# Layer 0's output projection by the seven-product scheme, and layer 1 begun with the second token half

## The chip, the cores and the metric

The program runs on one core of one Trainium2 chip. The metric is the device time of one execution in microseconds; the time of a kernel is the median of its runs. TensorE (PE) does the matmuls, VectorE (DVE), ScalarE (ACT) and GpSimd (POOL) everything between them, and SyncE (SP) issues most of the DMAs.

## What is computed

A decoder trunk of two layers over 1024 tokens of width 1024, all in float32. Each layer normalises, projects to eleven groups of columns, runs four mLSTM heads and four retention heads of width 256 in chunks, gates and normalises their outputs, and projects 2048 columns back to 1024:

```python
for l in range(DEPTH):                                   # DEPTH = 2
    ada = c_act @ w_ada[l] + b_ada[l]
    shift, scale, gate = jnp.split(ada, 3, axis=-1)
    h = rmsnorm(x, norm_g[l]) * (1.0 + scale[:, None, :]) + shift[:, None, :]
    p = h @ w_in[l]
    mq, mk, mv, mo, mz, mi, mf, rq, rk, rv, rz = split_cols(p)
    ...                                                  # conv, rotary, mLSTM and retention by chunks
    y_m = jax.nn.sigmoid(mo) * head_layernorm(cell, gn_m[l], N_HEADS_MLSTM) * jax.nn.silu(mz)
    y_r = head_layernorm(ret, gn_r[l], N_HEADS_RET) * jax.nn.silu(rz)
    y = jnp.concatenate([y_m, y_r], axis=-1) @ w_out[l]  # (1024, 2048) @ (2048, 1024)
    x = x + gate[:, None, :] * y
return rmsnorm(x, final_g)
```

The change is about the product with `w_out[0]`, the residual and the norm behind it, and the first projections of layer 1.

## The kernel before

**Numbers in two parts.** A float32 operand is split into a high part (rounded to the PE's format by ACT, a `CAST`) and the rest (a subtraction on DVE or POOL). One product of a 128x128 block with a 128x512 block is then three matmuls, `mm3`: high by high (L177), high by rest (L178), rest by high (L179). The buffers are pools: `b` has 59 tiles of 128x512, `acc` 12, `wH` 5 (high parts of weights), `R` 12 (raw weights and their rests). PSUM has eight banks of 128x512: four by `ps_p()` (named px and pz in the profile) and four by `ps_a()` (pa).

**Order.** PE's instructions stand in the order in which the program is written. The other engines are ordered by a scheduler at build time, except what goes through `late`, which keeps its place. Work beside the main stream is written as generators: `launch(gen, delay)` starts one, `tick()` is called after each unit of matmuls, and `yield n` waits for n ticks. So `yield` numbers and the table of steps `TABLE` decide where in PE's stream such work stands.

**The input projections** are done in pairs by a scheme of seven products instead of eight half-sized ones (`pair_product`, `vpair_product`): sums and differences of weight blocks and of blocks of the input (`build_forms`, by DVE at the start of a layer), seven products, and sums of their results. A `Feeder` loads, adds and splits weights some slots before each product.

**Attention.** `attention` runs the steps of `TABLE` for a head, one entry per tick: q, k, d, t, v are loads, Q, K, s splits, S scores, V values, U state updates. `gate_chain` makes the mLSTM gates at the start of each layer: cumulative sums on DVE, four transposes by PE (L562) of a tile T4, and a transfer through DRAM (`mdr`). `gate_rows` (layer 1 only) makes the gate row of the last residual; its matmul is L345.

**Layer 0's output projection.** `out_units(0, half, cc, ...)` makes, for one token half (512 tokens) and one half `cc` of the output columns, four banks of 128 columns x 512 tokens, in 16 units over k (128 input columns each) of four `mm3`: 4 x 16 x 4 x 3 = 768 matmuls. The order of the four quarters is (half 0, cc 0), (half 0, cc 1), (half 1, cc 0), (half 1, cc 1). `OutLoads` loads a weight block per unit, and for cc 0 also the normalised output and the gate of that k; DVE multiplies them (L1258), ACT scales and splits (L1261), DVE makes the rest (L1262), and the split tiles are kept for cc 1. The rest of a weight block (L408) goes to DVE for cc 0 and to POOL for cc 1. When a bank is done, `column_evac` adds it, times the gate, to the residual (L1309, DVE), squares it on ACT and adds up the squares (L1315, POOL, in the last quarter DVE).

**Into layer 1.** `norm_later` sums the squares over partitions by PE (L1372), makes the root on POOL, spreads it by PE (L1384) and scales the eight tiles of the half (DVE L144 for half 0, L1391 for half 1; ACT L1392, L1393; POOL L1394). Half 0's runs under the projection of half 1. Layer 1 begins with `first`: three column blocks of the input projection, 72 matmuls for half 0 (L1484, L1485, L1488) and then 72 for half 1, whose norm runs under those of half 0.

Of the kernel before, what the change touches and what calls it, by code (L numbers as in the profile page):

```python
# [12 lines left out]
F32R = mybir.dt.float32r  # L13
# [74 lines left out]
def tile_hybrid_trunk(ctx, tc, x, xt, c, positions, w_ada, b_ada, norm_g, w_in, w_blk, w_val, conv_w, conv_b,  # L88
# [20 lines left out]
    def bt(dt=F32, n=512):  # L109
        return big.tile([P, n], dt, tag="b", name=nm("b"))  # L110
# [219 lines left out]
    def gate_rows(l):  # L330
        for half in range(2):
            accs = []
            yield from ada_rows(l, 2 * D + half * 512, accs)
            brow = wt("acc", 512, NACC)
            Q.dma_start(brow[0:1, :], b_ada[l, 2 * D + half * 512:2 * D + (half + 1) * 512].unsqueeze(0))
            yield 1
            acc = accs[0]
            V.tensor_tensor(acc[0:1, :], acc[0:1, :], brow[0:1, :], ALU.add)
            yield 1
            a2 = (wt("wH", 512, NW, F32R), wt("R", 512, NR, F32R))  # L340
            split_to(a2, acc)
            yield 2
            pt = ps_a()
            for i in range(2):
                PE.matmul(pt, ones_r, a2[i], start=i == 0, stop=i == 1)  # L345
# [13 lines left out]
    def gate_cols(l, gcol):  # L359
        for half in range(2):  # L360
            accs = []
            yield from ada_rows(l, 2 * D + half * 512, accs)
            yield 2
            pt = ps_a()
            for i in range(4):
                PE.matmul(pt[:, i:i + 1], accs[0][:, i * P:(i + 1) * P], ones, start=True, stop=True)
            V.tensor_tensor(gcol[:, 4 * half:4 * half + 4], pt[:, 0:4],
                            cols[l][0][:, 120 + 4 * half:124 + 4 * half], ALU.add)
            yield 1
# [133 lines left out]
    def gate_chain(l, pgs, gt):  # L503
# [459 lines left out]
    def load_rotary(rot):  # L963
        for which in range(2):
            for i in range(2):
# [5 lines left out]
    busy = [False]  # L971
    TABLE = ("q0 k0 d0 t0", "", "v0", "Q0 K0 m0 d1", "s0 k1", "S0", "m1 q1 K1", "v1", "Q1", "V001 t1", "S1 k2 q2", "U01",
             "s1 d2 K2", "v2 Q2", "V10 U2 m2", "S2", "t2 d3", "V11 U3 k3", "s2 q3", "v3 K3", "Q3 m3", "V20 U4",
             "S3", "", "V21 U5", "", "", "", "V30", "V31", "")
# [328 lines left out]

    def column_evac(gcol, xn, sq, keep):
        def evac(half, cc, i, bank):
            ct = cc * 4 + i
            xr = bt()
            Q.dma_start(xr, xt[ct * P:(ct + 1) * P, half * HALF:(half + 1) * HALF])
            V.scalar_tensor_tensor(xr, bank, gcol[:, ct:ct + 1], xr, ALU.mult, ALU.add)  # L1309
            if ct == 0:  # L1310
                A.activation(sq, xr, AF.Square)
            else:
                o = wt("acc", 512, NACC)
                A.activation(o, xr, AF.Square)
                (V if half and cc else G).tensor_tensor(sq, sq, o, ALU.add)  # L1315
            xn[ct] = xr
            if cc == 0:
                keep(ct)
        return evac

# [38 lines left out]
    def row_rstd(ss, tag, rows=(0, 1, 2, 3)):  # L1359
# [6 lines left out]
        return [rs[:, tt:tt + 1] for tt in range(n)]  # L1366

    def norm_later(l, xn, sq, hT, half, keep, gaps):
        yield gaps[0]
        pt = ps_a()  # L1370
        for i in range(4):
# [4 lines left out]
        G.tensor_tensor(rs, s, mhalf, ALU.pow)  # L1376
        dg = bt()
        V.tensor_tensor(dg.rearrange("p (a b) -> p a b", a=4), ident.unsqueeze(1).to_broadcast([P, 4, P]),
                        rs.unsqueeze(2).to_broadcast([P, 4, P]), ALU.mult)
        for ct in range(4, KT):  # L1380
            keep(ct)
        yield gaps[1]
        pr = ps_a()
        PE.matmul(pr, f(ones_r), dg, start=True, stop=True)  # L1384
        R = bt()
        A.copy(R, pr)
        yield gaps[2]
        for k in range(KT):
            gain, shift = gsh[l][:, 0, k:k + 1], gsh[l][:, 1, k:k + 1]
# [76 lines left out]
    for l in range(DEPTH):  # L1466
# [10 lines left out]

        def first(half, k, parts=(0, 1)):
            hH, hL = hT[k][half]
            for i, w in enumerate(wf):  # L1480
                if 0 in parts:
                    if k == 0:
                        pf[i][half] = ps_p() if i < 2 else ps_a()
                    PE.matmul(pf[i][half], w[k][0], hH, start=k == 0, stop=False)  # L1484
                    PE.matmul(pf[i][half], w[k][1], hH, start=False, stop=False)  # L1485
            for i, w in enumerate(wf):
                if 1 in parts:
                    PE.matmul(pf[i][half], w[k][0], hL, start=False, stop=k == KT - 1)  # L1488

# [76 lines left out]
        else:  # L1566
            gr = gate_raw(l)
            for half in range(2):
                for k in range(KT):
                    first(half, k)  # L1570
                    tick()
                if half == 0:
                    drain()
                    wg = gate_weights(gr)
        for half in range(2):
# [55 lines left out]
        going, forms, left = {}, {}, {}  # L1631
        loads = OutLoads(l)
        for j, n, part in slots:
            left[j] = left.get(j, 0) + 1
        for j, n, part in slots:
# [6 lines left out]
            tick()  # L1642
            if sum(left.values()) == 5:
                loads.fetch(2)
            elif sum(left.values()) == 3:
                loads.make()
            left[j] -= 1
            if left[j] == 0 and jobs[j][0] == "k":
                launch(attention(l, jobs[j][1][0], gt), 4, 1)
        nhT = [[None, None] for _ in range(KT)]  # L1650
        if l == DEPTH - 1:
# [4 lines left out]
            for cc in range(2):  # L1656
                t = bt()
                Q.dma_start(t, final_g[cc * 512:(cc + 1) * 512].unsqueeze(0).to_broadcast([P, 512]))
                V.tensor_scalar(t, t, math.sqrt(D), None, ALU.mult)
                fg.append(t)  # L1660
        for half in range(2):
            if l < DEPTH - 1:
                xn, sq = [None] * KT, bt()
                keep = keep_rows(half, xn)
                evac = column_evac(gcol, xn, sq, keep)
                run_units(out_units(l, half, 0, loads, evac))
                run_units(out_units(l, half, 1, loads, evac, 2 if half else 0))
                launch(norm_later(l + 1, xn, sq, nhT, half, keep, (1, 2, 0) if half else (3, 3, 11)))
                continue
            xn = [[None, None] for _ in range(4)]  # L1670
# [46 lines left out]
```

## Time and profile before

| | us |
|---|---|
| median of three runs | 2266.18 (2264.73 to 2269.15) |
| the profiled execution | 2268.18 |
| its span in the profile | 2266.5 |
| PE, DVE, ACT, POOL busy | 2151.5, 1817.5, 1159.4, 964.3 |
| layer 0's output projection in the profile | 970 to 1161 |
| layer 1's `first` | 1161 to 1195 |
| mean granted PE clock | 0.979 |

A row of a view names line, engine, operation and tiles without their numbers; `b<-acc,cols,b` is a tile of the pool b made from three operands. A PE row's duration is from issue to the modelled end and overlaps its neighbours, so the pace of PE is read from the starts of rows that follow each other.

### The profile page before, as it was taken

The page shows a single profiled execution, that of the slowest core. Times are in us where ns is not written, and L with a number is a line of the kernel's source. Part 1 is how long each engine was busy: PE and PEld are TensorE (multiplying, and loading weights), DVE is VectorE, ACT ScalarE, POOL GpSimd, SP SyncE. Part 2 cuts the span into 40 slices and gives each one's busy share as a digit, 9 for nine tenths or more (in the row PEclk, how much of TensorE's full clock was granted, in tenths as well). Part 3 has the DMA queues.
Part 4 walks back from the last instruction along what each step waited for, and adds up shares of the span by engine and source line. Part 5 has one row for each costly group of instructions (what it writes and reads, how often), then busy time and mean ns, then how long its engine had stood idle before and what let it go on. Part 6 is the DMA issues. An engine that isn't in the chain of part 4 may idle for free.

```text
span 2266.5 us, 35156 instructions
## 1 busy us (share of the span) xinstructions
PE 2151.5 (95%) x11483; PEld 1832.0 (81%) x11483; DVE 1817.5 (80%) x3205; ACT 1159.4 (51%) x2163; POOL 964.3 (43%) x842
## 2 busy tenths in 40 slices
PE   7988999999999999999999799999999899999998
PEld 5787789878898878788778678988987888788886
DVE  6899888989979998784738989788797889977653
ACT  7634345444565656553555434543565565655442
POOL 1443244445454454424366235544544453442313
PEclk9999999999999999999999899999999999999999
DMA  8266688787686777686633767776866686686974
GB/s 285 61 176 186 188 230 249 215 235 202 185 247 175 194 203 186 175 270 210 225 107 84 214 185 210 214 198 185 245 166 192 175 238 186 173 216 203 261 245 118
DMA packets 452549, 448.31 MB, mean 198 GB/s; under 512 B 191219, under 2 KB 309755, under 8 KB 452365
## 3 DMA queue, kind: packets, MB, share of 16 engines
q1 hardware_dynamic: 432636, 410.14, 58.9%
q0 software_dynamic: 19584, 35.66, 10.4%
q8 instruction: 90, 1.47, 0.3%
q14 instruction: 95, 0.77, 0.1%
q10 hardware_dynamic: 144, 0.26, 0.0%
HBM read 322.69 MB, written 123.24 MB: 197 GB/s over the span
## 4 chain that ended last, share of the span: by engine, by line
PE 57%; DVE 22%; DMA 10%; issue 5%; POOL 2%; ACT 2%; SPq 1%; DVEq 0%; POOLq 0%; ACTq 0%
PE px L177 8%; PE px L178 8%; PE px L179 8%; PE pz L179 6%; PE pz L178 6%; PE pz L177 6%; PE pa L177 4%; PE pa L179 4%; PE pa L178 4%; DVE acc L881 3%; DVE R L408 2%; PE pa L1123 2%; DVE acc L626 2%; DMA acc<-kfr 1%; PE pa L1032 1%
## 5 line engine op out<-in xcount | busy, mean ns | idle before, releaser
L403 ACT CAST wH<-R 128x512 fp32r<-128x512 f32 x616 | 377.2, 617 | 476.6 <-PE px L178 133.0
L408 POOL TENSOR_TENSOR R<-R,wH 128x512 fp32r<-128x512 f32 x276 | 397.5, 1447 | 479.5 <-ACT wH L403 325.9
L177 PE MATMUL px<-b,wH 128*128 128x512 f32 x912 | 364.8, 400 | 8.2 <-ACT acc L767 7.4
L179 PE MATMUL px<-b,R 128*128 128x512 f32 x912 | 365.7, 401 | 0.0
L178 PE MATMUL px<-b,wH 128*128 128x512 f32 x912 | 364.8, 400 | 0.0
L408 DVE TENSOR_TENSOR R<-R,wH 128x512 fp32r<-128x512 f32 x340 | 257.2, 760 | 90.5 <-ACT wH L403 87.5
L178 PE MATMUL pz<-b,wH 128*128 128x512 f32 x704 | 280.2, 398 | 1.3 <-DVE b L1262 1.3
L179 PE MATMUL pz<-b,R 128*128 128x512 f32 x704 | 281.0, 399 | 0.0
L177 PE MATMUL pz<-b,wH 128*128 128x512 f32 x704 | 279.8, 397 | 0.2 <-ACT acc L767 0.2
L177 PEld LDWEIGHTS px<-b,wH 128*128 128x128 f32 x912 | 174.6, 191 | 48.1 <-ACT acc L767 8.9
L179 PEld LDWEIGHTS px<-b,R 128*128 128x128 f32 x912 | 174.0, 191 | 42.0 <-POOL R L408 0.8
L178 PEld LDWEIGHTS px<-b,wH 128*128 128x128 f32 x912 | 174.4, 191 | 39.3
L177 PE MATMUL px<-wH,b 128*128 128x256 f32 (+1 forms) x576 | 177.7, 309 | 27.4 <-DVE acc L824 12.3
L178 PE MATMUL px<-R,b 128*128 128x256 f32 (+1 forms) x576 | 174.9, 304 | 3.7 <-DVE R L408 3.7
L179 PE MATMUL px<-wH,b 128*128 128x256 f32 (+1 forms) x576 | 175.8, 305 | 0.0
L701 POOL DMA_DIRECT2D R<-in_w_blk_dram x104 | 92.1, 886 | 185.3 <-DMA R<-in_w_blk_dram 90.8
L178 PEld LDWEIGHTS pz<-b,wH 128*128 128x128 f32 x704 | 133.5, 190 | 32.0 <-DVE b L1262 2.2
L179 PEld LDWEIGHTS pz<-b,R 128*128 128x128 f32 x704 | 133.3, 189 | 31.5
L177 PEld LDWEIGHTS pz<-b,wH 128*128 128x128 f32 x704 | 133.8, 190 | 29.4 <-ACT acc L767 0.6
L177 PEld LDWEIGHTS px<-wH,b 128*128 128x128 f32 x576 | 115.5, 201 | 32.2 <-ACT acc L817 10.4
L179 PE MATMUL pz<-wH,b 128*128 128x256 f32 (+1 forms) x448 | 134.0, 299 | 0.4 <-DVE b L1262 0.4
L177 PE MATMUL pz<-wH,b 128*128 128x256 f32 (+1 forms) x448 | 134.0, 299 | 0.0
(357 smaller groups left out, 5346.7 us busy)
## 6 DMA issues: line engine op xcount, KB each, us to landing
R<-in_w_blk_dram SPq DMA_DIRECT2D x276, 256.0 KB
vdr<-acc SPq DMA_DIRECT2D x128, 256.0 KB
ring<-vdr SPq DMA_DIRECT2D x64, 512.0 KB
R<-in_w_out_dram SPq DMA_DIRECT2D x128, 256.0 KB
R<-in_w_blk_dram POOLq DMA_DIRECT2D x104, 256.0 KB, 4.7
R<-in_w_val_dram SPq DMA_DIRECT2D x80, 256.0 KB
gdr<-acc SPq DMA_DIRECT2D x64, 256.0 KB
acc<-in_w_ada_dram SPq DMA_DIRECT2D x64, 256.0 KB
```

What stands on the lines that cost most here:

```text
L177: PE.matmul(o, lt[0], rt[0], start=start, stop=False, skip_group_check=more)
L178: PE.matmul(o, lt[0], rt[1], start=False, stop=False, skip_group_check=more)
L179: PE.matmul(o, lt[1], rt[0], start=False, stop=stop, skip_group_check=more)
L403: A.copy(h, r)
L408: eng.tensor_tensor(lo, r, f(h), ALU.subtract)
L626: V.tensor_tensor(t, f(pair[0]), f(pair[1]), ALU.add)
L701: G.dma_start(raw[n], src, accum_op=ALU.add)
L881: V.scalar_tensor_tensor(acc[:, e:], pt[:, o + e - d:o + HALF - d], wcol, acc[:, e:], ALU.mult, ALU.add)
L1032: PE.matmul(pd, piece(kx[j], i, dt, tt * P, P), qd, start=dt == 0 and i == 0, stop=dt == 1 and i == 1)
L1123: PE.matmul(pi[:, 0:W], piece(qs[j], i, dt, tt * P, P), state[part][:, dt, 0:W], start=part + dt + i == 0, stop=ml and part + dt == 2)
```

## The change

The projection of layer 0 is done as two chunks of K, each a two by two product of blocks by seven products: columns k 8 to 15 (retention heads) in the first chunk, k 0 to 7 in the second; within a chunk the blocks are the lower and upper four k, the two halves of the output columns and the two token halves. The products come in the order `OUT`; each takes four slots (`kk`) of four `mm3`, so there are 2 x 7 x 4 = 56 slots of 12 matmuls, 672 in all. Four banks hold X, four Y and then Z; the second chunk swaps the two sets. `OutFeeder` makes the operands by slot: five weight blocks are loaded and one of each pair added by a DMA that accumulates (`wplus`, on POOL's queue), two more sums are made by DVE (L1351); the y tiles are multiplied (L1346), scaled by ACT, and combined to four differences (L1355, L1359); each slot's weight and y operand is split by ACT, the rest of the weight made by POOL, the rest of y by DVE, but by POOL in S1 (L1375). After the first of two products in a bank ACT copies the result (`keep`); with the second, DVE adds kept copy (L1461, `before`) and bank (L1469, `chain`) to the residual in each chunk, and in the second chunk squares are summed by DVE (L1479). Signs: the scheme here makes two of its sums negative, which half of the gate column (`gcol`) takes up.

Half 1 is finished by S4, one product ahead of half 0's a22. So `norm_later` of half 1 is launched under a22, and layer 1's `first` begins with half 1, its k in the order of `BORDER` (4 to 7, then 0 to 3), the rest parts one k behind the high parts; half 0 follows. PE row names shift: the sums are L1541, the spreading L1551, `first` L1654, L1655, L1658, scaling L1561.

Three more edits: in `TABLE` loads of k, q, d stand an entry or two earlier; in `gate_chain` layer 1's work begins three ticks earlier (9 for 12), the transfers of `mdr` come together later, and the transposes are three ticks later in layer 0 and at the same tick in layer 1; in `gate_rows` the matmul L345 comes three ticks later (5 for 2).

```diff
             split_to(a2, acc)
-            yield 2
+            yield 5
...
-        yield 12
+        yield 9 if l else 12
...
-            Q.dma_start(mdr[l][:, half * HALF:(half + 1) * HALF], mx[0:4])
...
-        yield 3
+        yield 2
+        for half in range(2):
+            Q.dma_start(mdr[l][:, half * HALF:(half + 1) * HALF], mxs[0:4, half * HALF:(half + 1) * HALF])
+        yield 4
...
-    TABLE = ("q0 k0 d0 t0", "", "v0", "Q0 K0 m0 d1", "s0 k1", "S0", "m1 q1 K1", "v1", "Q1", "V001 t1", "S1 k2 q2", "U01",
+    TABLE = ("q0 k0 d0 t0", "", "v0", "Q0 K0 m0 d1 k1", "s0", "S0 q1", "m1 K1", "v1", "Q1 d2", "V001 t1 k2", "S1 q2", "U01",
...
+    OUT = ("a11", "a12", "S2", "S1", "S3", "S4", "a22")
+    OUT_POOL = ('S1',)
+    class OutFeeder:
...
+            ev(t2 - 11 - early, wload, "S1", 0, 1)
+            ev(t2 - 9 - early, wplus, "S1", 1, 1)
...
+            ev(t2 - 5, lambda: ydiff("U1", "11", "12", y["11"]))
+            ev(t2 - 4, wsum, "S2", "a11", "S1")
...
+            for n in OUT:
+                ev(at[n] - 3, split, n, w, "w")
+                ev(at[n] - 2, rest, n, w, "w", G)
+                ev(at[n] - 3, lambda n=n: (y.__setitem__(n, y[yf[n]]), split(n, y, "y")))
+                ev(at[n] - 2, rest, n, y, "y", G if n in OUT_POOL else V)
...
+    SECOND = {"a12": (0, 0, "a11"), "S3": (1, 1, "S1"), "S4": (0, 1, "S2"), "a22": (1, 0, None)}
+    def out_strassen(feed, evac):
+        for chunk in range(2):
+            bank, keep = {}, {}
+            for n in OUT:
+                b = PRODUCT[n][0]
+                new = b not in bank
+                if new:
+                    bank[b] = [ps_p() if (b == "X") != bool(chunk) else ps_a() for _ in range(4)]
+                for kk in range(4):
+                    feed.step()
+                    w, y = feed.take((chunk, n, kk))
+                    for i in range(4):
+                        cs = slice(i * P, (i + 1) * P)
+                        mm3(bank[b][i], (w[0][:, cs], w[1][:, cs]), y, new and kk == 0, kk == 3, b != "Y")
...
+                if n in ("a11", "S1", "S2"):
+                    keep[n] = [wt("acc", 512, NACC) for _ in range(4)]
+                    for i in range(4):
+                        A.copy(keep[n][i], bank[b][i])
+                else:
+                    c, half, one = SECOND[n]
+                    launch(evac.chain(chunk, c, half, bank[b], keep[one] if one else None))
...
+            for half in (1, 0):
+                order = BORDER[half]
+                for n, k in enumerate(order):
+                    while hT[k][half] is None:
+                        tick()
+                    first(half, k, (0,), order)
+                    if n:
+                        first(half, order[n - 1], (1,), order)
                     tick()
...
+                launch(norm_later(1, xn, sq, nhT, half, keep, (2,1,1) if half else (4,2,0)))
+            out_strassen(loads, ColumnEvac(gcol, finished))
```

PE, at the sums of squares that the later of the norms begins with. Before, L1372 sums half 1's squares inside layer 1's `first` of half 0 (L1484, L1485, L1488):

```order
L1485 MATMUL pa_13255<-b_12924,R_13234 128x512
L1488 MATMUL pz_13249<-b_12925,wH_13225 128x512
L1488 MATMUL px_13252<-b_12925,wH_13229 128x512
L1488 MATMUL pa_13255<-b_12925,q_13212 128x512
L1372 MATMUL pa_13270<-ones,b_12383 128x1 x4
L1484 MATMUL pz_13249<-b_12948,wH_13225 128x512
```

Now half 1's squares are summed (L1541) inside the last product, a22 of the second chunk, after two of its four slots:

```order
L177 MATMUL pa_12557<-b_13129,wH_13127 128x512
L178 MATMUL pa_12557<-b_13130,wH_13127 128x512
L179 MATMUL pa_12557<-b_13129,R_13146 128x512
L1541 MATMUL pz_13217<-ones,b_13054 128x1 x4
L177 MATMUL pa_12554<-b_13151,wH_13149 128x512
L178 MATMUL pa_12554<-b_13152,wH_13149 128x512
```

What moved: before, 18 matmuls of `first` stand between the end of the projection and these sums; now 24 matmuls of a22 stand between the end of S4 and them.

DVE, in the projection. Before, between the evacuations of the first and of the second quarter (L1309), the whole of its work for 16 units:

```order
L1309 SCALAR_TENSOR_TENSOR b_12037<-px_11428,gsh_353,b_12037 128x512
L1324 STREAM_TRANSPOSE acc_12043<-b_12037 128x512
L1258 TENSOR_TENSOR acc_12273<-acc_12272,acc_12273 128x512
L1262 SCALAR_TENSOR_TENSOR b_12334<-acc_12273,cols_495,b_12333 128x512
L1258 TENSOR_TENSOR acc_12295<-acc_12294,acc_12295 128x512
L1258 TENSOR_TENSOR acc_12317<-acc_12316,acc_12317 128x512
```

Now, around the evacuation of the first chunk's a22 (L1469), a stretch of some four slots:

```order
L1375 TENSOR_TENSOR b_12583<-b_12204,b_12582 128x512
L1355 TENSOR_TENSOR b_12148<-b_12148,b_12280 128x512
L1375 TENSOR_TENSOR b_12606<-b_12241,b_12605 128x512
L1351 TENSOR_TENSOR b_12151<-b_12151,R_12277 128x512
L1469 SCALAR_TENSOR_TENSOR b_12303<-pz_11511,gsh_353,b_12303 128x512
L1346 TENSOR_TENSOR b_12372<-acc_12371,b_12372 128x512
L1469 SCALAR_TENSOR_TENSOR b_12305<-px_11512,gsh_353,b_12305 128x512
L1469 SCALAR_TENSOR_TENSOR b_12307<-pz_11513,gsh_353,b_12307 128x512
L1359 SCALAR_TENSOR_TENSOR b_12654<-b_12148,b_12362 128x512
```

What moved: evacuations, rests of y, sums and products of y now stand mixed on DVE through the whole projection, where before it had 13 instructions for the second quarter.

SP's queue, at the first loads for the projection. Before, two loads of `w_out` stand ahead of head 3's second half of keys (`kdr`, `kfr`):

```order
L398 DMA R_11256<-in_w_out_dram 128x512
L398 DMA R_11262<-in_w_out_dram 128x512
L848 DMA gdr_3_0_1_136<-acc_11036 128x512
L905 DMA acc_11244<-kdr_3_1_194 32x8x64 x4
```

Now fifteen loads for `OutFeeder` stand there, the last of them these:

```order
L1340 DMA b_11343<-gdr_5_1_0_145 128x512
L1339 DMA acc_11227<-ndr_4_0_99 128x512
L1339 DMA acc_11233<-ndr_4_0_99 128x512
L1333 DMA b_11346<-in_w_out_dram 128x512
L1333 DMA R_11386<-in_w_out_dram 128x512
L851 DMA gdr_3_0_0_135<-acc_10987 128x512
L908 DMA acc_11259<-kdr_3_1_194 32x8x64 x4
```

What moved: the keys, and the query load behind them, come about a dozen transfers later in the queue.

More of the change, by code (lines that the diff above doesn't have):

```diff
@@ new lines, in tile_hybrid_trunk, with __init__, ahead, before @@
+    class ColumnEvac:
+        def __init__(self, gcol, finished):
+            self.gcol, self.finished = gcol, finished
+            self.xn = [[None] * KT for _ in range(2)]
+            self.sq = [None, None]
+            self.keeps = [keep_rows(half, self.xn[half]) for half in range(2)]
+        def ahead(self, chunk, n):
+            if chunk == 0 and n in ("a11", "S1", "S2", "S4"):
+                c, half, _ = SECOND[{"a11": "a12", "S1": "S3", "S2": "S4", "S4": "a22"}[n]]
+                for i in range(4):
+                    ct = c * 4 + i
+                    xr = self.xn[half][ct] = bt()
+                    Q.dma_start(xr, xt[ct * P:(ct + 1) * P, half * HALF:(half + 1) * HALF])
+        def before(self, c, half, keep):
+            for i in range(4):
+                ct = c * 4 + i
+                xr, g = self.xn[half][ct], self.gcol[:, ct:ct + 1]
+                V.scalar_tensor_tensor(xr, keep[i], g, xr, ALU.mult, ALU.add)
+                if i % 2:
+                    yield 1
+        def chain(self, chunk, c, half, banks, keep):
+            for i in range(4):
+                ct = c * 4 + i
+                xr, g = self.xn[half][ct], self.gcol[:, ct:ct + 1]
+                V.scalar_tensor_tensor(xr, banks[i], g, xr, ALU.mult, ALU.add)
+                if chunk == 0:
+                    continue
+                last = (c == 0) == bool(half)
+                if self.sq[half] is None:
+                    self.sq[half] = bt()
+                    A.activation(self.sq[half], xr, AF.Square)
+                else:
+                    o = wt("acc", 512, NACC)
+                    A.activation(o, xr, AF.Square)
+                    V.tensor_tensor(self.sq[half], self.sq[half], o, ALU.add)
+                if not last:
+                    self.keeps[half](ct)
+            if chunk and last:
+                self.finished(half, self.xn[half], self.sq[half], self.keeps[half])
+            return
+            yield
@@ L1476, in tile_hybrid_trunk, with first @@
         pf = [[None, None] for _ in wf]
-        def first(half, k, parts=(0, 1)):
+        def first(half, k, parts=(0, 1), order=range(KT)):
             hH, hL = hT[k][half]
@@ L1487, in first @@
                 if 1 in parts:
-                    PE.matmul(pf[i][half], w[k][0], hL, start=False, stop=k == KT - 1)
+                    PE.matmul(pf[i][half], w[k][0], hL, start=False, stop=k == order[-1])
         if l == 0:
@@ L1642, in tile_hybrid_trunk @@
             tick()
-            if sum(left.values()) == 5:
+            left[j] -= 1
+            rest = sum(left.values())
+            if l and rest == 4:
                 loads.fetch(2)
-            elif sum(left.values()) == 3:
+            elif l and rest == 2:
                 loads.make()
-            left[j] -= 1
+            elif not l and rest == 5:
+                loads = OutFeeder(l, -6)
+            elif not l and rest < 5:
+                loads.step()
             if left[j] == 0 and jobs[j][0] == "k":
```

151 lines of the change are left out of this document (108 added, 43 removed).

## The prediction

> **What bounds the kernel now.** The first view is the page: each engine's busy time, then the chain that ended last.
>
> ```profile
> PE 2151.5 (95%) x11483; PEld 1832.0 (81%) x11483; DVE 1817.5 (80%) x3205; ACT 1159.4 (51%) x2163; POOL 964.3 (43%) x842
> PE 57%; DVE 22%; DMA 10%; issue 5%; POOL 2%; ACT 2%; SPq 1%; DVEq 0%; POOLq 0%; ACTq 0%
> ```
>
> PE is busy 95% of 2266.5 us, and DVE carries over a fifth of the chain. These shares mix stages, so the second view cuts out three: the projection, layer 1's `first`, and the start of layer 1 up to its gate transposes. The columns are the window, its length, then busy time of PE, weight loads, DVE, ACT and POOL, the granted PE clock, DMA share and GB/s.
>
> ```profile
> 970.00:1161.00 191.00, 189.01 (x841) 152.78 (x840) 106.92 (x169) 88.29 (x145) 78.88 (x59) 1.00 0.66 217
> 1161.00:1195.00 34.00, 33.42 (x147) 26.53 (x146) 18.27 (x24) 17.62 (x29) 19.90 (x15) 1.00 0.28 88
> 1195.00:1310.00 115.00, 100.52 (x566) 84.21 (x565) 105.64 (x136) 62.11 (x99) 53.42 (x38) 0.91 0.54 150
> ```
>
> The projection is PE's: 189.0 of 191.0 us at full clock, DVE free for 84. In the third stretch DVE is the fuller engine (105.6 of 115) and PE stands for 14. The third view is PE's list of waits between 940 and 1420 us (total, times, longest):
>
> ```profile
> PE pa L345 <- ACT wH L868: 4.0, 1, 4.0
> PE pa L562 <- DVE cL L144: 3.0, 1, 3.0
> PE pz L178 <- DVE b L1262: 1.3, 2, 1.2
> PE pa L1372 <- DVE b L1315: 0.6, 1, 0.6
> PE pa L345 <- POOL R L869: 0.6, 1, 0.6
> ```
>
> Projection and `first` cost 1.9 us of waits together. So fewer matmuls pay in full there, as long as DVE, ACT, POOL and the loads keep pace.
>
> **Term 1: matmuls.** The timeline of PE gives the pace; 24 matmuls lie between these two starts:
>
> ```profile
> 1120.26 0.39 PE L177 MATMUL pa<-b,wH 128*128 128x512 f32 x1
> 1125.86 0.39 PE L177 MATMUL pa<-b,wH 128*128 128x512 f32 x1
> ```
>
> 5.60/24 = 0.2333 us each, 2.80 us per slot of twelve. 768 - 672 = 96 matmuls: **-22.4 us**. Nothing hides that, since PE is the limit of this stage.
>
> **Term 2: DVE against PE inside the projection.** From the first slot of S2 (slot 8) to the first of the second a22 (slot 52) PE needs 44 x 2.80 = 123.2 us. In the changed order DVE has, over that distance, 119 instructions with two operands from SBUF (products, differences, sums, rests of y), 24 from PSUM, 8 transposes and some 3 us of small ones; POOL has 52 of two operands and ten accumulating DMAs to issue. Prices from the timelines of DVE and POOL in today's projection (start, duration):
>
> ```profile
> 1158.92 0.68 DVE L1315 TENSOR_TENSOR b<-b,acc 128x512 f32<-128x512 f32 x1
> 1159.66 0.75 DVE L1309 SCALAR_TENSOR_TENSOR b<-pa,gsh,b 128x512 f32<-128x512 f32 x1
> 1119.74 0.71 DVE L1324 STREAM_TRANSPOSE acc<-b 128x512 f32<-128x512 f32 x1
> 1120.38 12.96 DVE L144 TENSOR_TENSOR b<-b,b 128x512 f32<-128x512 f32 x8
> 1122.53 1.74 POOL L408 TENSOR_TENSOR R<-R,wH 128x512 fp32r<-128x512 f32 x1
> 1141.97 1.28 POOL L1394 TENSOR_TENSOR b<-b,b 128x512 fp32r<-128x512 f32 x1
> ```
>
> The two-operand instruction has no single price: 0.68 us alone, 12.96/8 = 1.62 where POOL runs two-operand work back to back, and POOL's goes from 1.28 to 1.74. What a mixture costs is shown by the groups of DVE (first four) and POOL between 1195 and 1310 us (busy, mean ns | idle before):
>
> ```profile
> L626 DVE TENSOR_TENSOR acc<-b,b 128x512 f32<-128x512 f32 x20 | 22.5, 1175 | 0.0
> L408 DVE TENSOR_TENSOR R<-R,wH 128x512 fp32r<-128x512 f32 x16 | 12.4, 787 | 4.0 <-ACT wH L403 3.9
> L705 DVE TENSOR_TENSOR R<-R,R 128x512 f32<-128x512 f32 x8 | 8.5, 1060 | 0.1
> L309 DVE SCALAR_TENSOR_TENSOR acc<-acc,cact,acc 128x512 f32<-128x512 f32 x7 | 5.7, 808 | 1.7 <-DMA acc<-in_w_ada_dram 1.6
> L869 POOL TENSOR_TENSOR b<-acc,b 128x512 fp32r<-128x512 f32 x16 | 25.8, 1635 | 13.8 <-ACT b L868 13.8
> L408 POOL TENSOR_TENSOR R<-R,wH 128x512 fp32r<-128x512 f32 x11 | 18.8, 1715 | 9.5 <-ACT wH L403 6.8 <-issue 1.4 <-DVE R L408 1.3
> ```
>
> (22.5 + 12.4 + 8.5 + 5.7)/51 = 0.963 us, beside 27 POOL instructions in 115 us. Over the whole run the rests of weights on DVE average less:
>
> ```profile
> L408 DVE TENSOR_TENSOR R<-R,wH 128x512 fp32r<-128x512 f32 x340 | 257.2, 760 | 90.5 <-ACT wH L403 87.5
> ```
>
> The other instructions cost 24 x 0.75 + 8 x 0.71 + 3 = 26.7 us. DVE's total is then 107.6 us at 0.68, 117.1 at 0.76, 141.3 at 0.963, and 156.5 if 52 of the 119 pay 1.62 and 67 pay 0.68. Against 123.2 and the two slots' lead (5.6) with which rests are made, PE's lag is 0, 0, 141.3 - 123.2 - 5.6 = 12.5, and 27.7. I take **+12.5**: that stretch is the nearest in kind, and POOL's density here (52 in 123 us) is above its 27 in 115, so not the cheap end.
>
> A page speaks against the change here. The Trainium skill, "SBUF — State Buffer", section "SBUF: two separate sides", says that a DVE instruction with two SBUF inputs and a GpSimd instruction that reads SBUF lock each other out, the second waiting for the whole of the first. By that a colliding DVE instruction would last 0.68 + 1.28 = 1.96 us, and 52 of them would make the lag 45.4. The rows above show 1.62 at worst and 0.963 in the mixture, so the sum does not use it.
>
> **Term 3: the handover to layer 1.** Half 1's sums of squares (L1541) stand 24 matmuls, 5.6 us, behind S4. Before them DVE has four evacuations, a rest and four additions: 4 x 0.75 + 5 x 0.963 = 7.8 us, a wait of 2.2 (0.8 with additions at 0.68; 5.5 at 1.62). Then `first` reads the tiles in turn. Between the first and fifth scaling DVE has four evacuations, four transposes and six two-operand instructions, 3.0 + 2.8 + 5.8 = 11.6 us, against 33 matmuls, 7.7: another 3.9 (2.2 to 7.8). Today's wait at L1372 (0.6) goes. **+5.5** (2.4 to 12.7).
>
> **Term 4: gate transposes and gate row.** Layer 0's gate transposes are in the list of waits of the whole run, layer 1's and the gate row in the timeline, in brackets what each waited for:
>
> ```profile
> PE pa L562 <- DVE cL L144: 7.4, 2, 4.4
> 1297.31 1.11 PE L562 MATMUL pa<-ident,cL 128*128 128x128 f32 x4 [3.00 <-DVE cL L144]
> 1302.42 0.79 PE L345 MATMUL pa<-wH,ones_r 128*128 128x512 f32 x1 [4.01 <-ACT wH L868]
> 1300.00:1320.00 20.00, 16.98 (x63) 12.87 (x64) 10.65 (x19) 9.98 (x18) 9.35 (x8) 0.82 0.74 201
> ```
>
> At stake: 4.4 + 3.0 + 4.0 + 0.6 = 12.0 us, and the clock of 0.82 behind them (20 x 0.18 = 3.6). Three ticks of nine or twelve matmuls are over 6 us, more than any of these waits, so layer 0's goes in full, -4.4. In layer 1 the work starts three ticks earlier and the transposes keep their tick; but DVE is the fuller engine there, and moving a PE instruction does not make DVE faster. I take half of 7.6, -3.8, and -1 of the clock: **-9.2** (-15.6 to 0).
>
> **Term 5: loads.** The tile view of `w_out` gives SP's transfers (min/median/max ns, first to last):
>
> ```profile
> L398 SPq DMA_DIRECT2D R<-in_w_out_dram x128: 327/333/2345, 946.4 to 2233.1; - x128
> ```
>
> Head 3's last keys and query come a dozen transfers later in SP's queue: 12 x 0.333 = 4.0 us. The other heads' loads stand one or two ticks earlier in `TABLE`, which can gain as much: **0** (-4 to +4). Their cover is the ticks between load and use.
>
> **Term 6: `first`.** Today DVE idles 15.7 of the 34 us of `first`. Now, from a22's evacuations up to the first scaling of half 0, its order holds four evacuations, eight transposes and twelve two-operand instructions: 3.0 + 5.7 + 12 x 0.68 to 0.963 = 16.9 to 20.3 us, against 72 matmuls of half 1, 16.8. So half 0's tiles come up to 3.5 us late, less what the waits of term 3 have already let DVE catch up, and up to 8 where these instructions collide (12 x 0.4 more). **+2** (0 to +8).
>
> The gate column's sign, the kept copies (ACT has 103 us free in the projection) and eight banks each with one owner: 0.
>
> **Sum.** -22.4 + 12.5 + 5.5 - 9.2 + 0 + 2 = -11.6. The profiled execution took 2268.18 us, so 2256.6; it lies 2.0 above the median of 2266.18, so **2254.6** beside the median. The rivals below are given in the same terms. All cheap ends together: -22.4 + 0 + 2.4 - 15.6 - 4 + 0 = -39.6, 2226.6. All dear ends: -22.4 + 27.7 + 12.7 + 0 + 4 + 8 = +30, 2296.2.
>
> **Rivals.**
>
> *DVE becomes the bound of the projection (slower).* Every rest of y waits behind DVE's sums and products, each of PE's slots behind a rest. With collisions at 1.62: -22.4 + 27.7 + 12.7 - 4.4 + 4 (term 6) = +17.6, **2283.8**. It decides once term 2 passes 24.1 (where the forecast's sum reaches zero): (123.2 + 5.6 + 24.1 - 26.7)/119 = 1.06 us for the mean two-operand instruction. For it: 1.62 and 1.175 in the rows, POOL's density. Against it: 0.76 over the whole run, and instructions that wait for loads and splits leave gaps in which they do not collide.
>
> *DVE keeps pace (much faster).* At 0.76 term 2 is 0; with term 3 at 2.4, term 4 at -13.0, term 6 at 0: -33.0, **2233.2**. For it: DVE is free 84 us in this stage today, and 0.76 is a mean over 340 instructions. Against it: POOL is far less busy over the run (43%) than 52 x 1.6 = 83 us in 123 here.
>
> *The saving is spent where DVE already bounds.* The stretch of 1195 to 1310 has DVE at 92%. PE arrives earlier and stands longer at the same DVE instructions: term 4 is 0, head 3's loads cost 4: -22.4 + 12.5 + 5.5 + 0 + 4 + 2 = +1.6, **2267.8**, no change.
>
> **How the numbers follow.** Forecast 0.45, DVE bound 0.20, DVE keeps pace 0.20, spent 0.15. A measurement of this kernel tells some 0.2%, 4.5 us, from no change. The forecast's case reaches across 2261.7 in about a tenth of its width and the third rival reaches both ways: faster 0.62 (0.40 + 0.20 + 0.02), same 0.13 (0.03 + 0.10), slower 0.25 (0.20 + 0.02 + 0.03). The range leaves out half of each outer case, 0.10 each: 2231 to 2281. The faster cases' own range is 2231 to 2261.
>
> **What would show it.** Term 1: the pace of 2.80 us per slot where nothing waits, 672 matmuls of `mm3`. Term 2: mean of DVE's L1375, L1346 and L1355 (0.96 forecast; under 0.8 the second rival, over 1.06 the first), and PE's waits for DVE `b` L1375, some 12 us in total. Waits for POOL `R` L1375 or for a DMA of `wplus` would be a limit that the sum does not have. Term 3: waits at L1541, L1654 and L1658, some 6 us. Term 4: the waits at L562 and L345 gone or halved. Term 5: no new wait on keys or queries of head 3. The forecast is wrong if the projection with `first` (225 us today) is not shorter, by some 2 to 10 us, while the rest of the run gains some 9.

## The result, and the profile after

The changed kernel takes 2303.32 us (2300.73 to 2307.16), the kernel before, run beside it, 2265.45: a ratio of 1.0166 (95% interval 1.0146 to 1.0186), 38 us slower where 12 us faster was forecast. Its profiled execution has a span of 2298.9 us, 32.4 over the 2266.5 of before. Stage times below are read from one profiled execution of a kernel, which in the experiments lies up to 12 us from the median of its runs. The page of the kernel after, busy time by engine:

```profile
PE 2133.5 (93%) x11387; PEld 1810.1 (79%) x11387; DVE 1938.8 (84%) x3287; ACT 1188.4 (52%) x2233; POOL 1023.2 (45%) x880
```

The 96 matmuls are gone from PE, and PE's busy time fell by 18.0 us. DVE's rose by 121.3 us, although it has only 82 instructions more: 1.48 us for each. Where the span grew is read from the starts of PE's rows at the same places of the program in both traces (us):

| stretch | before | after |
|---|---|---|
| start to layer 0's first scores | 310.3 | 309.5 |
| to head 3's last scores of layer 0 | 619.8 | 623.4 |
| from there to layer 1's `first`: the projection, with the end of head 3 in it | 230.8 | 251.3 |
| `first` | 36.6 | 47.7 |
| to layer 1's gate transposes | 99.9 | 103.1 |
| from there to PE's last matmul | 960.8 | 955.1 |

The loss is 20.5 us in the projection and 11.1 us in `first`, with differences of 0.8 to 5.7 us elsewhere. Of the 20.5, 6.9 arise before the first slot (46.7 us after head 3's last scores, 39.8 before). The windows of the kernel after, cut at the first slot, at the first slot of S2, at the last a22 and at `first` (busy time of PE, weight loads, DVE, ACT, POOL; clock, DMA share, GB/s):

```profile
979.60:1022.00 42.40, 30.97 (x146) 24.27 (x145) 42.30 (x62) 23.57 (x44) 24.00 (x17) 0.97 0.97 295
1022.00:1159.70 137.70, 128.71 (x541) 101.14 (x541) 135.29 (x155) 75.88 (x139) 90.85 (x61) 0.98 0.46 147
1159.70:1184.40 24.70, 16.01 (x61) 12.56 (x60) 17.08 (x22) 8.91 (x17) 11.66 (x9) 0.79 0.33 108
1184.40:1232.00 47.60, 38.46 (x157) 29.14 (x157) 32.82 (x39) 30.44 (x48) 29.35 (x21) 0.96 0.29 94
```

Now DVE is busy 177.6 of the 180.1 us up to the last a22, and PE stands. PE's waits from 931 to 1232 us, the longest groups:

```profile
PE pz L1541 <- DVE b L1479: 8.7, 1, 8.7
PE pa L178 <- DVE b L1375: 8.7, 4, 3.4
PE pz L178 <- DVE b L1375: 5.0, 3, 2.6
PE pz L1654 <- ACT b L1562: 4.5, 3, 2.1
PE pa L1541 <- DVE b L1479: 4.1, 1, 4.1
PE pa L1126 <- ACT b L1347: 3.7, 1, 3.7
```

They are the rests of y (L1375), the sums of squares at the two handovers (L1541), and the scaled tiles (L1654). Also ACT's L1347, behind which head 3 waits, follows DVE's product L1346. Why DVE is full is seen in its timeline with POOL's beside it (start, duration; three rows of DVE, then one of POOL):

```profile
1134.99 0.68 DVE L1375 TENSOR_TENSOR b<-b,b 128x512 fp32r<-128x512 f32 x1
...
1137.30 3.49 DVE L1461 SCALAR_TENSOR_TENSOR b<-acc,gsh,b 128x512 f32<-128x512 f32 x2
1140.71 3.47 DVE L1375 TENSOR_TENSOR b<-b,b 128x512 fp32r<-128x512 f32 x2
...
1135.20 11.82 POOL L1375 TENSOR_TENSOR R<-b,wH 128x512 fp32r<-128x512 f32 x7 [0.68 <-POOL R L1375]
```

The same instruction takes 0.68 us alone and 3.47/2 = 1.74 us while POOL makes seven rests of weights at 11.82/7 = 1.69 each. Such rows of DVE overlap by some 0.07 us in the profile (the next one starts 1.70 after), so their durations add up to more than the time for which DVE is busy.

### The profile page after: what moved, and what is told of

It is laid out like the page before. It is cut to its first block, busy times and chain, and to the rows that moved or that the text cites. A ratio compares the mean times of both kernels' runs of the same rounds, so it can differ in the third digit from the quotient of the medians.

```text
span 2298.9 us, 35165 instructions
## 1 busy us (share of the span) xinstructions
PE 2133.5 (93%) x11387; PEld 1810.1 (79%) x11387; DVE 1938.8 (84%) x3287; ACT 1188.4 (52%) x2233; POOL 1023.2 (45%) x880
## 5 line engine op out<-in xcount | busy, mean ns | idle before, releaser
L409 POOL TENSOR_TENSOR R<-R,wH 128x512 fp32r<-128x512 f32 x244 | 353.0, 1454 | 425.7 <-ACT wH L404 266.2
L404 ACT CAST wH<-R 128x512 fp32r<-128x512 f32 x552 | 336.9, 617 | 357.3 <-PE px L178 81.1
L177 PE MATMUL px<-b,wH 128*128 128x512 f32 x904 | 361.9, 400 | 13.5 <-ACT acc L770 8.4
L409 DVE TENSOR_TENSOR R<-R,wH 128x512 fp32r<-128x512 f32 x308 | 239.6, 780 | 61.7 <-ACT wH L404 59.4
L178 PE MATMUL pz<-b,wH 128*128 128x512 f32 x696 | 276.1, 397 | 5.0 <-DVE b L1375 5.0
L177 PE MATMUL pz<-b,wH 128*128 128x512 f32 x696 | 275.0, 395 | 0.0
L177 PEld LDWEIGHTS px<-b,wH 128*128 128x128 f32 x904 | 173.0, 191 | 54.2 <-ACT acc L770 10.5
L177 PE MATMUL px<-wH,b 128*128 128x256 f32 (+1 forms) x576 | 175.2, 304 | 28.3 <-DVE acc L827 18.7
L179 PE MATMUL px<-wH,b 128*128 128x256 f32 (+1 forms) x576 | 173.1, 301 | 0.2 <-DVE b L1265 0.2
L177 PEld LDWEIGHTS pz<-b,wH 128*128 128x128 f32 x696 | 131.5, 189 | 28.1 <-DVE acc L780 0.3
L872 POOL TENSOR_TENSOR kc<-acc,kc 128x512 fp32r<-128x512 f32 x64 | 92.4, 1444 | 112.0 <-ACT kc L871 92.3
L177 PE MATMUL pz<-wH,b 128*128 128x256 f32 (+1 forms) x448 | 135.2, 302 | 7.4 <-ACT acc L602 6.3
L177 PEld LDWEIGHTS px<-wH,b 128*128 128x128 f32 x576 | 112.7, 196 | 33.2 <-DVE acc L827 10.1
```

What stands on the lines that cost most here:

```text
L177: PE.matmul(o, lt[0], rt[0], start=start, stop=False, skip_group_check=more)
L178: PE.matmul(o, lt[0], rt[1], start=False, stop=False, skip_group_check=more)
L179: PE.matmul(o, lt[1], rt[0], start=False, stop=stop, skip_group_check=more)
L404: A.copy(h, r)
L409: eng.tensor_tensor(lo, r, f(h), ALU.subtract)
L872: eng.tensor_tensor(dst[1], src, f(dst[0]), ALU.subtract)
```

## Experiments

Times are medians beside runs of the kernel before on the same chip (2267 to 2269 us), and ratios are to those. Line numbers of a kernel can differ by one to five from those above.

**Is it the side edits?** `e1_no_side` puts all three back, `e2_side_only` puts them alone into the kernel before, `f3_table_only` puts back TABLE alone.

```diff
-            yield 5
+            yield 2
...
-    TABLE = ("q0 k0 d0 t0", "", "v0", "Q0 K0 m0 d1 k1", "s0", "S0 q1", "m1 K1", ...
+    TABLE = ("q0 k0 d0 t0", "", "v0", "Q0 K0 m0 d1", "s0 k1", "S0", "m1 q1 K1", ...
```

> The changed kernel with its three side edits (TABLE, gate_chain, gate_rows) as they were before. Theory A (VectorE is full in the projection: two-operand instructions slowed by POOL's, PE waiting for them and then running at a lower clock): the slowdown stays, 2295 to 2306 us against 2303 for the changed kernel. Theory B (the side edits and the shifted loads make head 3 and the start of layer 1 late): 10 us or more come back, 2285 to 2293, and PE's waits of 8.5 us before the first slot and of 3.7 at L1126 go.

> The kernel before with the three side edits alone. Theory A: 2263 to 2270 us, within 4 us of the kernel before. Theory B: slower by 10 us or more, 2275 to 2280. The prediction's term 4 would be 9 us faster, 2257.

> The changed kernel with only TABLE as it was before, the edits in gate_chain and gate_rows kept. If the 9 us that e1_no_side gave come from the loads of head 3 standing elsewhere, the same here: 2290 to 2297 us, projection about 245 us. If they come from the gate edits, 2300 to 2306.

Measured: 2294.41 us, ratio 1.0118 (1.008 to 1.0156); 2270.73, ratio 1.0007 (0.9992 to 1.0023); 2288.39, ratio 1.009 (1.0072 to 1.0107). So alone the edits do nothing that the runs can tell. With the new projection, undoing all three gives 9 us and undoing TABLE alone 15; these two intervals overlap, so TABLE carries the cost and the gate edits none that can be told. Neither theory had edits that cost only together with the new projection. By the starts of PE's rows, with TABLE back the first slot comes 43.1 us after head 3's last scores instead of 46.7, and the rest of the projection takes 201.4 instead of 204.6. SP issues head 3's last keys 24.7 us after those scores with TABLE back, and 31.9 in the changed kernel. That this is how TABLE costs time was not tried, nor which of the moved loads does it.

**Does POOL's work make DVE's dearer?** `e3_rests_dve` gives the rests of weights to DVE, `e4_no_wrest` leaves them out.

```diff
-                ev(at[n] - 2, rest, n, w, "w", G)
+                ev(at[n] - 2, rest, n, w, "w", V)
```
```diff
-                    forms[kind, n][1] = wt("R", 512, NR, F32R)
+                    forms[kind, n][1] = forms[kind, n][0]
+                    return
```

> The changed kernel with the rests of the weights in the projection (49 instructions) on VectorE instead of POOL. If a POOL instruction of two operands holds VectorE up by about as much as VectorE would need to do it itself, VectorE's mean two-operand instruction falls from 0.99 to 0.72 us, its total from 149.5 us for 151 to about 144 for 200, and the time stays within 10 us of 2303. If POOL's help is real (instructions cost VectorE 0.7 to 0.8 us whatever POOL does), 49 x 0.76 = 37 us come on top: 2335 to 2345.

> The changed kernel without the rests of the weights in the projection: the third matmul of each mm3 reads the high part instead, so PE's work is the same and POOL has 49 instructions less; the output lacks those low parts. Theory A: VectorE's two-operand instructions fall to 0.70 us, 44 us of VectorE's time in the projection go, and with them the waits for L1375 (14 us), most of the 8.7 us at L1541 and the slower pace behind them (10 us): 2265 to 2280. Theory B: 2298 to 2306.

Measured: 2289.66 us, ratio 1.009 (1.0056 to 1.0124), and 2277.67, ratio 1.0034 (1.0016 to 1.0052). The edits take all 56 rests of weights, one per slot, where the expectations speak of 49. Giving DVE 56 instructions more made the kernel some 14 us faster, more than the 10 that the first case allowed. DVE's groups between 990 and 1160 us, first of the changed kernel (rests of y, kept copies, differences), then of `e3_rests_dve` (the same three, and the rests of weights it took over):

```profile
L1375 DVE TENSOR_TENSOR b<-b,b 128x512 fp32r<-128x512 f32 x42 | 39.6, 955 | 0.0
L1461 DVE SCALAR_TENSOR_TENSOR b<-acc,gsh,b 128x512 f32<-128x512 f32 x24 | 29.4, 1260 | 0.1
L1355 DVE TENSOR_TENSOR b<-b,b 128x512 f32<-128x512 f32 x16 | 17.2, 1090 | 0.0
```
```profile
L1375 DVE TENSOR_TENSOR b<-b,b 128x512 fp32r<-128x512 f32 x43 | 30.3, 718 | 0.0
L1461 DVE SCALAR_TENSOR_TENSOR b<-acc,gsh,b 128x512 f32<-128x512 f32 x24 | 17.1, 737 | 0.0
L1355 DVE TENSOR_TENSOR b<-b,b 128x512 f32<-128x512 f32 x16 | 11.9, 744 | 0.0
L1375 DVE TENSOR_TENSOR R<-b,wH 128x512 fp32r<-128x512 f32 x35 | 23.5, 677 | 4.1 <-ACT wH L1368 4.1
```

The durations of all DVE rows with two operands from SBUF, from the first L1375 to the projection's end: 172 rows in 171.8 us (0.999 each) beside 73 on POOL; in `e3_rests_dve` 227 in 164.0 us (0.723 each) beside 16. So a rest on POOL cost DVE (171.8 - 172 x 0.723)/56 = 0.85 us, more than the 0.7 us for which DVE makes it itself. The rule of the Trainium skill that the prediction weighed ("SBUF — State Buffer", section "SBUF: two separate sides") agrees in kind; its full block would be POOL's 1.28 us for each, and 0.85 was measured. `e4_no_wrest` brings the price to 0.747 as well (167 rows, 15 on POOL) and the projection from 251.3 to 221.5 us, but leaves `first` at 47.8: the handover is another loss.

**Are the two costs separate, and is DVE's total the bound?** `e5_both` joins `e1_no_side` and `e3_rests_dve`; `e7_less_dve` takes 38 more instructions off DVE.

```diff
-                V.scalar_tensor_tensor(xr, keep[i], g, xr, ALU.mult, ALU.add)
+                pass
...
-                    V.tensor_tensor(self.sq[half], self.sq[half], o, ALU.add)
+                    pass
```

> The changed kernel with the side edits undone and the rests of the weights on VectorE. If the two costs are separate, both come off: 2303 - 9 - 14 = 2280 us, 12 us above the kernel before. If they are the same waits seen twice, 2286 to 2292.

> The kernel e5_both without the 24 additions of kept copies (L1461) and without the 14 sums of squares (L1479), so 38 instructions or some 27 us less for VectorE; its output lacks them, PE's work is the same. If VectorE is the bound of projection and `first`: waits for L1375 gone, the projection at 215 us or under (245 with side edits undone, 239 with rests on VectorE), `first` at 42, and 20 us or more under e5_both. If ACT, POOL or loads take its place: less than 8 us.

Measured: 2282.57 us, ratio 1.0069 (1.0045 to 1.0093). The median lies nearer to 2280 than to 2286, so the costs are separate for the most part; but by ratios two separate costs would give 1.0166 - 0.0048 - 0.0076 = 1.0042, just under the interval, and one cost seen twice 1.009, just inside it, so this is not settled. And 2257.09, ratio 0.9955 (0.9937 to 0.9972): 25.5 us for an estimated 27 us of DVE's work. The projection falls to 215.8 us and `first` to 42.9, and the waits for rests are nearly gone (PE, 930 to 1240 us of `e7_less_dve`):

```profile
PE pz L178 <- DVE b L1373: 2.6, 2, 1.4
...
PE pa L178 <- DVE b L1373: 0.8, 1, 0.8
```

So DVE keeps pace here, but only because work is left out, and even then the kernel is 10 us faster than before (0.45%) and not 33 as in the prediction's case of that name. From the first slot to `first` PE takes 175.0 us, 16.0 less than before's 191.0 where 22.4 of matmuls went, and `first` still takes 6.3 us more than before.

**The handover.** All four build on `e5_both`. `e6_sums_pe` adds up the last four squares by PE, and transposes half 1's last four tiles later. `e8_half1_early` finishes half 1 two products before the end (its operands are made in the new order too, and `first` takes k from 0 to 7 in both halves), `e8_norm_sooner` also launches half 1's norm a slot earlier (5 below, 6 in `e8_half1_early`), `e9_both_handover` is `e8_half1_early` with PE's sums. The first cut is from `e8_norm_sooner`, the second from `e6_sums_pe`.

```diff
     OUT = ("a11", "a12", "S2", "S1", "S3", "S4", "a22")
+    OUTS = (OUT, ("a11", "S1", "S2", "S4", "S3", "a12", "a22"))
...
-                launch(norm_later(1, xn, sq, nhT, half, keep, (2,1,1) if half else (4,2,0)))
+                launch(norm_later(1, xn, sq, nhT, half, keep, (5,1,1) if half else (4,2,0)))
```
```diff
-                    V.tensor_tensor(self.sq[half], self.sq[half], o, ALU.add)
+                    if last:
+                        self.more[half].append(o)
+                    else:
+                        V.tensor_tensor(self.sq[half], self.sq[half], o, ALU.add)
...
-            PE.matmul(pt[:, i:i + 1], sq[:, i * P:(i + 1) * P], ones, start=True, stop=True)
+            for j, q in enumerate(sq):
+                PE.matmul(pt[:, i:i + 1], q[:, i * P:(i + 1) * P], ones, start=j == 0, stop=j == len(sq) - 1)
```

> The kernel e5_both with the last four squares of each half added up by PE (20 matmuls of one column instead of 4, accumulating in PSUM) and not by VectorE, and half 1's last four kept tiles transposed just before their own scaling instead of after the first. If the handover to layer 1 is late because the sums stand behind VectorE's backlog, L1541's waits (4.6 and 4.1 us) fall to under 2 each, `first` goes from 48 to about 41 us, and the time is 6 to 10 us under e5_both. If the chain sums, root, spreading, scaling itself is too long for the work that covers it, less than 3 us.

> The kernel e5_both with the products of the second chunk in the order a11, S1, S2, S4, S3, a12, a22: half 1 is finished two products (22.4 us) before the end instead of one, and its sums of squares stay at the same place of PE's stream, after two slots of a22. If `first` loses its 11.8 us because half 1's evacuations and sums have only one product as cover, L1541's wait for half 1 (4.6 us) goes, `first` falls from 48 to 42 us, and the time is 6 to 10 us under e5_both (2282.6), 2273 to 2277. If VectorE's total work is what counts, the waits only move: within 4 us of e5_both.

> The kernel e8_half1_early with half 1's norm launched one slot sooner: its sums stand after one slot of a22. If scaling then is what `first` waits for (L1654 for ACT, 4.6 us in e5_both), 2 to 4 us under e8_half1_early; if VectorE is still behind with a12's evacuation there, the wait at L1541 grows by as much.

> The kernel e8_half1_early with the last four squares of each half added up by PE as in e6_sums_pe. If half 0's sums (L1541, 4.1 us) are the handover's other half, 3 to 5 us under e8_half1_early; if not, within 2 us, as e6_sums_pe against e5_both.

Measured: 2284.4 us (ratio 1.0074, 1.005 to 1.0097), 2278.09 (1.006, 1.0039 to 1.0081), 2274.6 (1.0036, 1.0016 to 1.0055), 2278.61 (1.0077, 1.0046 to 1.0108). PE's sums remove the waits at L1541 and give nothing: `first` goes from 48.4 to 47.0 us only. The new order alone is 4.5 us under `e5_both` by the medians, 2 by the ratios, whose intervals overlap: no gain that can be told. The wait of half 1's sums is gone there, PE waits 5.3 us for ACT's split instead (L177 for `b` L1367), and `first` stays at 49.2. With the earlier launch the medians differ by 8.0 us, the ratios by 7.5, and `first` falls to 43.2: the waits for scaled tiles (L1652) go, and of the two for sums one shrinks and one grows (`e5_both`, then `e8_norm_sooner`, L1539 and L1544 being L1541):

```profile
PE pz L1539 <- DVE b L1477: 4.6, 1, 4.6
PE pz L1652 <- ACT b L1560: 4.6, 3, 2.1
PE pa L1539 <- DVE b L1477: 4.1, 1, 4.1
```
```profile
PE pa L1544 <- DVE b L1482: 5.1, 1, 5.1
...
PE pz L1544 <- DVE b L1482: 3.0, 1, 3.0
```

This is the best version found that computes the reference, still above the kernel before (`first` 36.6).

**Taking real work off DVE.** `f1_keep_by_dma` is `e8_norm_sooner` with the kept copies added by accumulating DMAs.

```diff
-                        A.copy(keep[n][i], bank[b][i])
+                        ct = SECOND[{"a11": "a12", "S1": "S3", "S2": "S4"}[n]][0] * 4 + i
+                        A.activation(keep[n][i], bank[b][i], AF.Copy, scale=evac.gcol[:, ct:ct + 1])
...
-                V.scalar_tensor_tensor(xr, keep[i], g, xr, ALU.mult, ALU.add)
+                G.dma_start(xr, keep[i], accum_op=ALU.add)
```

> The kernel e8_norm_sooner with the 24 additions of kept copies (L1461) taken off VectorE: ACT scales the copies by the gate as it makes them, and an accumulating DMA on POOL's queue adds each to the residual. VectorE loses 24 x 0.715 = 17 us of the projection's 167. If VectorE's total is still the bound, waits for L1375 and L1544 (14 us together) shrink by half and the time falls by 6 to 12 us, 2263 to 2269, level with the kernel before or better. If the DMAs land late, or POOL's issues (24 x 0.95 us) hold VectorE up as its arithmetic does, within 3 us of 2274.6.

Measured: 2284.59 us, ratio 1.007 (1.0046 to 1.0095), 10 us slower than `e8_norm_sooner`. DVE's price stays (205 rows with two SBUF operands at 0.719 us; 229 at 0.726 in `e8_norm_sooner`), and DVE has 24 rows less, so the gain is lost elsewhere. PE's waits:

```profile
PE pa L1124 <- DVE b L1473: 11.1, 1, 11.1
...
PE pz L178 <- POOL b L1374: 4.5, 1, 4.5
```

Head 3's matmul at L1124 needs the bank that the first evacuation (L1473) frees. The accumulating DMAs take 3.3 to 8.7 us from issue to landing (median 5.4), but they are not what that evacuation waits for: the four ahead of it had landed by 1012.30 us, and it starts at 1016.89. It stands in DVE's queue behind a product that waits for a load of y, and five rows more:

```profile
1013.27 0.69 DVE L1345 TENSOR_TENSOR b<-acc,b 128x512 f32<-128x512 f32 x1 [3.91 <-DMA b<-gdr]
```

In the projection DVE waits 15.3 us for such loads, 5.7 in `e8_norm_sooner`. Why they land later and why the scheduler puts the evacuation behind them was not tried.

**The slower pace behind a wait.** `f4_warm_wait` puts 100 useless matmuls in front of half 1's sums in the changed kernel.

```diff
+        if half:
+            for i in range(100):
+                PE.matmul(pt[:, 0:128], ones_r, ones_r, start=True, stop=True)
```

> The changed kernel with 100 small matmuls (128x128) of no use ahead of half 1's sums of squares, in the place where PE waits 8.7 us. If the pace behind the wait (granted clock 0.52 in the 6 us after it) is lowered because PE stood idle, the clock there is near 1.0 and the time 1 to 4 us lower, 2299 to 2302; if it is lowered for another reason, the clock stays near 0.5 and the time is the same or up to 3 us higher.

Measured: 2304.46 us, ratio 1.0165 (1.0145 to 1.0186): the same as the changed kernel. But the clock (third number from the end) in the six us behind the wait is another; the changed kernel, then `f4_warm_wait`:

```profile
1174.00:1180.00 6.00, 5.77 (x18) 4.96 (x19) 1.03 (x3) 0.00 (x0) 2.33 (x2) 0.52 0.31 90
```
```profile
1174.00:1180.00 6.00, 6.00 (x33) 4.79 (x33) 0.98 (x3) 1.20 (x2) 2.13 (x2) 1.00 0.02 6
```

So the clock of 0.52 came from standing idle. What curing it is worth, this run doesn't show, for the useless matmuls last longer than the wait that they fill (`f4_warm_wait`: PE, then DVE's last sums of squares, done at 1165.67 + 5.11 = 1170.78 us, then PE's sums):

```profile
1163.22 11.38 PE L1542 MATMUL pz<-ones_r 128*128 128x128 f32 x100
1165.67 5.11 DVE L1479 TENSOR_TENSOR b<-b,acc 128x512 f32<-128x512 f32 x4
1174.44 1.00 PE L1544 MATMUL pz<-ones,b 128*128 128x1 f32 x8
```

PE's sums start 3.7 us after their operand is ready, and behind them PE reaches `first` in 7.4 us instead of 10.0: the 2.6 us that the clock gave, the matmuls had taken.

## Why the prediction was wrong, step by step

**Where the 44 us lie.** By stretch, forecast and measured, in us: to the first scores -4.4 and -0.8; heads 0 and +3.6; projection -7.7 (terms 1 and 2 and the wait at L1541) and +20.5; `first` +5.3 and +11.1; from there on -4.8 and -2.5. So 28.2 of the miss are in the projection.

**What bounds it.** The reading of before holds: PE was the limit there. The forecast let DVE fall 12.5 us behind in one stretch; in fact DVE was the limit of the whole stage. The rival "DVE becomes the bound", at 0.20 and 2283.8 us, is right in kind, but not for its reason: it needed a mean price over 1.06 us. From S2 to the last a22 the mean over all DVE rows with two operands from SBUF was 118.2/116 = 1.02 us, and the rows that the prediction named as its sign (L1375, L1346, L1355) came out at (34.7 + 14.6 + 14.1)/66 = 0.96, just as forecast.

**Term 1** is right: 96 matmuls, -22.4 us.

**Term 2** comes out near for the stretch it counts, and is too short as a term. From S2 to the last a22 it forecast 123.2 + 12.5 us; measured are 137.7, a lag of 14.5. The price there was 1.02 us against 0.963. That the lag came so near is in part luck: the sum adds up durations that overlap (all rows of DVE there add up to some 147 us, and it was busy 135.3), and it counts a lead of 5.6 us that DVE did not have. The step that failed is its start: it took DVE as free at slot 8. In the eight slots before, DVE is busy 42.30 of 42.40 us, with head 3's last steps beside the feeder's first products and rests, and PE needs 42.4 us for 28.2 us of matmuls (96 of 0.2333, and some 50 narrower ones of head 3 at 0.12): 14.2 us that stand in no term.

**Term 3** failed by the same assumption. It costed the handover as if DVE began it on time: a wait of 2.2 us at L1541. Measured: 8.7 us, and 24.7 us for the last a22, whose 48 matmuls need 11.2 us and some 0.9 for the sums. Of the loss of 12.6 us, 8.7 are the wait and the rest a slower pace (clock 0.79). `first` then takes 11.1 us more (forecast 3.9 and 2 of term 6). `e7_less_dve` shows that 5.5 of these are DVE's load (48.4 to 42.9); `e8_norm_sooner` saves 5.2 by the order and an earlier launch together. Some 6 us no run removed.

**Term 4** failed. Up to layer 0's first scores 0.8 us are gained, not 4.4, and `e2_side_only` shows that the edits alone give nothing. The waits that the prediction named as its sign, at L562 and L345, have vanished from the list, as it said; but PE's waits from 0 to 320 us show, before and then after:

```profile
PE px L177 <- DVE acc L824: 7.4, 1, 7.4
PE pa L562 <- DVE cL L144: 4.4, 1, 4.4
PE px L178 <- DVE R L408: 1.9, 2, 1.5
```
```profile
PE px L177 <- DVE acc L827: 9.9, 2, 7.4
PE px L178 <- DVE R L409: 4.7, 3, 2.7
```

The 4.4 us went to the next instructions that need DVE: 2.5 and 2.8 us more. The third rival says this of layer 1's start, where the stretch up to the gate transposes took 3.2 us more, where 1.5 less were forecast (half of 3.0). What follows is 5.7 us shorter, but it is also 4.0 and 5.8 us shorter in `e5_both` and `e7_less_dve`, which lack the edits.

**Term 5** was wrong in size: 0 (-4 to +4) for what costs 9 to 15 us together with the new projection. Its 0.333 us is SP's time to issue a load, and SP also waits between its issues. Head 3's last keys are issued, before and then after:

```profile
949.30 1.90 SPq L905 DMA_DIRECT2D acc<-kdr  x4
```
```profile
964.82 2.20 SPq L908 DMA_DIRECT2D acc<-kdr  x4
```

That is 19.2 and 31.9 us behind head 3's last scores: 12.7 us later, where 4.0 were counted. How much of the loss comes from this was not settled.

**Range.** The ends of DVE's price were wide enough, and its signs (DVE's price, the waits for rests, the vanished waits of term 4) came out as forecast. What was missing is that the terms are not separate. One queue carries the backlog from stage to stage, so its lateness enters each of them.

## What to carry to other kernels

When a change shifts work from PE to DVE, add up DVE's whole queue over the whole stage, with what the neighbouring stages leave in it, and not stretch by stage from zero; 38 instructions off that queue gave 25.5 us here, nearly their own duration. Work handed from a full DVE to POOL was no help here: a two-operand instruction on POOL cost DVE more (0.85 us) than doing it there (0.7 us). A wait that vanishes from the list need not be a gain: PE may stand as long at the next instruction that needs the same engine, as at the start of layer 0.

## What the runs showed of the hardware

DVE's and POOL's two-operand instructions in step take about 1.7 us each (0.68 and 1.3 alone). PE's granted clock was 0.52 behind an idle time of 8.7 us and 1.00 where small matmuls filled it. 24 accumulating DMAs of 256 KB between tiles in SBUF took 3.3 to 8.7 us from issue to landing.
